# A hybrid decoder step on one core: fewer unread products, gate tiles over both PSUM pools, two output weights loaded earlier, four operand sums on another engine

## The chip, the cores and the metric

The kernel runs on one NeuronCore of a Trainium2 chip. The metric is the device time of one execution in microseconds (us). The engines are called by the names of the profile: PE (TensorE, the matrix products; PEld is its weight load), DVE (VectorE), ACT (ScalarE), POOL (GpSimd) and SP (SyncE, which here only issues transfers).

## The reference, cut to what matters

1088 tokens (1024 of a prompt and 8 sequences of 8) go through one layer, with D = 1024 and a feed-forward width of 2816:

```python
h = rmsnorm(x, pre_mix_g)
proj = h @ w_in                      # q, k, v, g of 4 retention heads; q, k, v, o of 4 mLSTM heads; 8 gate columns
ret_y = head_groupnorm(retention_chunked(q_r, k_r, v_r, S)) * silu(g_r)
ml_y = head_groupnorm(mlstm_chunked(q_m, k_m, v_m, i_pre, f_pre, C, n, m)) * sigmoid(o_m)
x = x + rmsnorm(concat(ret_y, ml_y) @ w_out, post_mix_g)
up = rmsnorm(x, pre_ffn_g) @ w_up    # then a causal convolution of width 3 over the tokens
ffn = (gelu(gate) * val) @ w_down
x = x + rmsnorm(ffn, post_ffn_g)     # the states and the last rows of `up` are outputs too
```

Everything is fp32.

## The kernel before, in words

**Tiles.** Tokens lie in the free dimension, in four blocks of 272 (`BLK`); a contraction over 1024 is eight k-tiles of 128. An fp32 product is made of three products of rounded operands: `split_to` (L141) writes the rounded part of an operand on ACT (L144) and the remainder on DVE (L146), and `dense` (L157) issues, for each k-tile, high x high, low x high and high x low (L165), 24 matmuls of 128x272 for a weight tile and a block. `load_w` (L149) brings one weight tile of 512 KB in and splits it; the high part is then named wh, the low part wl (in the output projection also woh, wol).

**The start.** `idle(n)` (L152) issues n products of a constant tile into a bank that nothing reads: 20 at the kernel's start (L239), and 3 after each of the first eight real products of the first projection (L442 passes the 3 to `dense`, which calls `idle` after each k-tile). The first projection makes two tiles of values at once. Block 0 of x becomes the operands hh (ACT, L205) and hl (DVE, L206).

**The projections** (`proj`, L431). Each of 32 weight tiles is multiplied with four blocks; each product takes a PSUM bank (by default of the pool psA, which has 2 banks; psB has 6 and serves the heads), and a callback reads the bank. For values that is a copy on ACT (L453), for q and k a rotation (`q_r`, `k_r`), for a gate tile `early_gate` (L479): DVE scales the bank into z (L484), ACT takes the sigmoid, DVE multiplies (L487). The four retention gate tiles are projected in one run (loop at L540 in `front`/`mix_head`), and among them DVE makes the mLSTM's running sums over rows of 4x1088 (`gate_rows`, L354 to L426, with scans at L383 and L394). The last four projections (L790 to L793) are those of the mLSTM gates (`late_gate`, L490, z at L497); the last one has `mix_split` (L780) as its `done`: after each block it splits the finished mixer output into the output projection's operands mh (ACT L787) and ml (DVE L788).

**The output projection** (`out_proj`, L838). All eight PSUM banks go to a new pool, psF, at L796. Eight weight tiles st_out are loaded by `load_wo` (L824), one ahead of the products and one more ahead of each; tiles 0 to 3 get buffers of their own, 4 to 7 (woh, wol) others. Each product is read on ACT (mo L847, oacc L849) and added on DVE (L851).

**The feed-forward part** is one level of Strassen's scheme: 22 tiles of gate and value, in pairs, with sums of operands. `pair_out` (L1029) makes, for each pair, the product act of gelu(gate) and value (DVE L1034), sends it to memory as bd, makes four sums of halves of it on POOL (L1042) and sends those too (L1044). `prep_a` (L1150) makes sums of the down weights wd on POOL (L1158). `halves` (L1135) splits operands for the down products: rb, read back from bd, and ra_*, from wd, on ACT (L1137) and DVE (L1138). The down products dn are L1209 to L1211.

**The order.** A scheduler orders the instructions of each engine when the kernel is built; `issue_after` only adds constraints. Each engine then runs its list strictly in order, and waits at an instruction for its inputs and its buffers.

Of the kernel before, what the change touches and what calls it, by code (L numbers as in the profile page):

```python
# [10 lines left out]
F32 = mybir.dt.float32  # L11
# [3 lines left out]
ALU = mybir.AluOpType  # L15

P = 128
D = 1024
# [74 lines left out]
def hybrid_layer_kernel(ctx: ExitStack, tc: tile.TileContext, a: dict, o: dict):  # L93
# [47 lines left out]
    def split_to(x, hi, lo, eng=nc.vector, after=None):  # L141
        act, dve = after or (None, None)
        with tc.issue_after(act.ins) if act else nullcontext():
            nc.scalar.activation(hi, x, AF.Copy)  # L144
        with tc.issue_after(dve.ins) if dve and eng is nc.vector else nullcontext():
            eng.tensor_tensor(lo, x, hi.bitcast(F32), ALU.subtract)  # L146
        return hi, lo
# [9 lines left out]
    def dense(ps, w, x, b, term=None, wait=0):  # L157

        hi, lo = w
        for k in range(KT):  # L160
            ws = slice(k * P, (k + 1) * P)
            xh, xl = (t[:, k % 4, qcols(b)] for t in x[b // 2][k // 4])
            for i, (u, v) in enumerate(((hi, xh), (lo, xh), (hi, xl))):
                if term in (None, i):
                    nc.tensor.matmul(ps, u[:, ws], v, start=k == i == 0, stop=k == KT - 1 and i == 2)  # L165
            idle(wait)
# [72 lines left out]
    idle(20)  # L239
# [191 lines left out]
    def proj(*jobs, mid=None, done=None, banks=lambda i, b: psA, terms=None):  # L431

        ws = [j[2] if len(j) > 2 else load_w(a["wi"][j[0]], f"in{j[0]}") for j in jobs]
        for b in range(4):
# [5 lines left out]
            if b == 0:  # L440
                for i, term in terms or ():
                    dense(pss[i], ws[i], h, b, term, 3 if i == term == 0 else 0)  # L442
# [64 lines left out]
    def mix_head(hd, ml):  # L507
# [15 lines left out]
        else:  # L523
# [12 lines left out]
            if hd == 0:  # L536
# [3 lines left out]
                for i in range(NH):  # L540
                    proj((12 + i, early_gate(i)))
# [238 lines left out]
    def mix_split(b):  # L780
# [3 lines left out]
        for k in range(0, KT, 2):  # L784
            hi, lo = (t[:, k % 4:k % 4 + 2, qcols(b)] for t in mx[b // 2][k // 4])
            x = yT[k // 2][:, :, o0:o0 + n]
            nc.scalar.activation(hi, x, AF.Copy)  # L787
            nc.vector.tensor_tensor(lo, x, hi.bitcast(F32), ALU.subtract)  # L788
# [4 lines left out]
    proj((31, late_gate(7)), done=mix_split)  # L793
# [18 lines left out]
    wtag = [0]  # L812
# [9 lines left out]
    wo = []  # L822

    def load_wo():  # L824

        m = len(wo)
        if m in (4, 6):
            wx.extend(slot(m + 4 + i, f"wo{'hl'[i]}{m}").rearrange("p k n -> p (k n)") for i in range(2))
        if m < 4:
            wo.append(load_w(a["wo"][m], f"out{m}", *wtile()))  # L830
        elif m < KT:
            hi, lo = (t[:, m % 2 * D:(m % 2 + 1) * D] for t in wx[-2:])
            wo.append(split_to(stage_w(a["wo"][m], f"out{m}"), hi, lo))

    wx = []
# [193 lines left out]
    def pair_out(j, ug, uv):  # L1029
# [11 lines left out]
        for o_, x, y in ((e0, e1, e0), (e1, o1, e1), (o1, o1, e0), (o0, o0, o1)):  # L1041
            nc.gpsimd.tensor_tensor(o_, x, y, ALU.subtract)  # L1042
# [343 lines left out]
```

## Time and profile before

| | |
|---|---|
| median of 3 runs (lowest to highest) | 1390.55 us (1388.64 to 1392.19) |
| the profiled execution's own time | 1391.41 us |
| its span in the profile | 1389.6 us |
| mean granted TensorE clock | 0.993 |
| PE busy | 1355.2 us (98%), 10633 products |
| DVE, ACT, POOL busy | 1006.3 us (72%), 596.1 us (43%), 445.6 us (32%) |

Busy times count what an engine executes; a wait is idle time ahead of an instruction, put down to what released it. The windows view cuts the span into stretches and gives for each the busy time of every engine and the granted clock, PEclk, as a share of 2.4 GHz: 0.50 is the lower level, 1.2 GHz, all through. Adjacent products overlap in the timeline: one takes some 0.29 us and the next begins some 0.125 us after it.

### The profile page before, as it was taken

What the parts mean: (1) busy time and instruction counts of PE and PEld (TensorE: products, weight loads), DVE (VectorE), ACT (ScalarE), POOL (GpSimd) and SP (SyncE); (2) the same over time, 40 slices, a digit from 0 to 9 for tenths busy, and PEclk for the clock granted to TensorE, in tenths of its full rate; (3) what the DMA queues carried; (4) which work ended last, traced back from release to release, by engine and by line L of the source; (5) the groups of instructions that cost most, each with busy time, mean ns of one, the idle gap of its engine ahead of it and who ended that gap; (6) DMA issues with size and microseconds to landing.
All of it is one profiled execution on the core that took longest, in us unless ns stands there. A gap on an engine that the chain in (4) does not pass through costs nothing.

```text
span 1389.6 us, 27023 instructions
## 1 busy us (share of the span) xinstructions
PE 1355.2 (98%) x10633; PEld 1329.6 (96%) x10633; DVE 1006.3 (72%) x2009; ACT 596.1 (43%) x1107; POOL 445.6 (32%) x571
## 2 busy tenths in 40 slices
PE   9999999999999999899899999999999999999995
PEld 9999999999999999899899999999999999999995
DVE  6786775476374366467989878778777787896677
ACT  7443433312222235446464434344334354553553
POOL 0444440388666000000343322221222206782000
PEclk9999999999999999999999999999999999999998
DMA  6433441376886210433224444433444458533363
GB/s 240 137 122 116 162 139 46 111 230 209 189 174 206 63 48 31 158 99 96 93 79 147 140 148 140 140 126 122 141 148 138 135 165 286 179 114 96 93 214 129
DMA packets 93167, 192.82 MB, mean 139 GB/s; under 512 B 16240, under 2 KB 41456, under 8 KB 92528
## 3 DMA queue, kind: packets, MB, share of 16 engines
q1 hardware_dynamic: 80736, 149.03, 33.1%
q0 software_dynamic: 12160, 41.95, 10.5%
q8 instruction: 84, 1.38, 0.4%
q14 instruction: 43, 0.35, 0.1%
q10 hardware_dynamic: 144, 0.11, 0.0%
HBM read 134.58 MB, written 56.47 MB: 137 GB/s over the span
## 4 chain that ended last, share of the span: by engine, by line
PE 86%; DVE 7%; ACT 3%; DMA 2%; issue 2%; SPq 0%; DVEq 0%; ACTq 0%
PE in L165 25%; PE up_S L1014 6%; PE up_S L1013 6%; PE up_S L1012 6%; PE out L165 5%; PE dn L1211 5%; PE dn L1209 5%; PE dn L1210 4%; PE up_A L1013 4%; PE up_A L1012 4%; PE up_A L1014 4%; DMA x<-in_x 1%; PE up_A L1057 1%; PE up_A L1058 1%; PE up_A L1056 1%
## 5 line engine op out<-in xcount | busy, mean ns | idle before, releaser
L165 PE MATMUL in<-hh,wh_in 128*128 128x272 f32 x1024 | 301.9, 296 | 5.2 <-DVE z L484 4.0
L165 PE MATMUL in<-hh,wl_in 128*128 128x272 f32 x1024 | 297.3, 293 | 0.0
L165 PE MATMUL in<-hl,wh_in 128*128 128x272 f32 x1024 | 296.7, 292 | 0.0
L165 PEld LDWEIGHTS in<-hh,wh_in 128*128 128x128 f32 x1024 | 193.4, 189 | 8.5 <-DVE z L484 2.7
L165 PEld LDWEIGHTS in<-hh,wl_in 128*128 128x128 f32 x1024 | 193.2, 190 | 5.4 <-issue 5.1
L165 PEld LDWEIGHTS in<-hl,wh_in 128*128 128x128 f32 x1024 | 192.8, 189 | 0.8 <-issue 0.8
L144 ACT ACTIVATE wh_up<-st_up 128x1024 fp32r<-128x1024 f32 x84 | 80.6, 959 | 170.2 <-PE up_S L1013 104.4
L1138 DVE TENSOR_TENSOR rb<-rb 128x544 fp32r<-128x544 f32 x78 | 74.7, 963 | 40.9 <-ACT rb L1137 40.4
L146 DVE TENSOR_TENSOR wl_up<-st_up,wh_up 128x1024 fp32r<-128x1024 f32 x84 | 94.7, 1127 | 9.6 <-ACT wh_up L144 9.6
L986 DVE TENSOR_TENSOR Uv<-Uv,up_S 128x272 f32<-128x272 f32 (+1 forms) x200 | 66.8, 376 | 47.3 <-PE up_S L1014 47.3
L1042 POOL TENSOR_TENSOR act<-act 128x544 f32<-128x544 f32 x44 | 70.3, 1598 | 77.4 <-DMA bd<-act 52.8
L736 POOL TENSOR_TENSOR tab<-tab 128x256 f32<-128x256 f32 x104 | 79.4, 774 | 14.3 <-DMA tab<-in_wu 9.8
L1158 POOL TENSOR_TENSOR wd<-wd 128x512 f32<-128x512 f32 x44 | 72.0, 1663 | 32.8 <-DMA wd<-in_wd 19.9
L1137 ACT ACTIVATE rb<-rb 128x544 fp32r<-128x544 f32 x78 | 50.5, 650 | 73.2 <-DMA rb<-bd 64.5
L1027 DVE SCALAR_TENSOR_TENSOR c<-Uv,vec,c 128x1024 f32<-128x1024 f32 (+1 forms) x88 | 70.2, 800 | 8.9 <-ACT c L1025 8.9
L977 POOL MEMSET Ug<- 128x2 f32 x22 | 2.2, 99 | 227.8 <-DVE yT L500 111.3
L736 POOL TENSOR_TENSOR wq<-wq 128x256 f32<-128x256 f32 x56 | 54.5, 984 | 44.7 <-DMA wq<-in_wu 42.4
L1027 DVE SCALAR_TENSOR_TENSOR c<-Ug,vec,c 128x1024 f32<-128x1024 f32 x88 | 67.5, 807 | 1.5 <-ACT c L1025 1.5
L736 POOL DMA_DIRECT2D tab<-in_wu x52 | 36.8, 713 | 79.1 <-DVE k_r L468 59.6
L1025 ACT ACTIVATE c<-Ug,vec 128x1024 f32<-128x1024 f32 (+1 forms) x44 | 34.6, 834 | 47.1 <-DVE Ug L990 44.4
L146 DVE TENSOR_TENSOR wl_in<-st_in,wh_in 128x1024 fp32r<-128x1024 f32 (+2 forms) x33 | 40.9, 1238 | 14.5 <-ACT wh_in L144 14.4
L1014 PE MATMUL up_S<-T1h,wl_up 128*128 128x272 f32 x160 | 46.6, 292 | 0.0
(547 smaller groups left out, 4678.7 us busy)
## 6 DMA issues: line engine op xcount, KB each, us to landing
rb<-bd SPq DMA_DIRECT2D x76, 272.0 KB, 2.9
st_up<-sd SPq DMA_DIRECT2D x40, 512.0 KB, 3.9
bd<-act SPq DMA_DIRECT2D x33, 544.0 KB, 4.6
st_in<-in_wi SPq DMA_DIRECT2D x31, 512.0 KB, 4.2
tab<-in_wu POOLq DMA_DIRECT2D x52, 256.0 KB, 5.2
sd<-tab POOLq DMA_DIRECT2D x26, 512.0 KB, 3.8
st_up<-in_wu SPq DMA_DIRECT2D x24, 512.0 KB, 3.6
wd<-in_wd SPq DMA_DIRECT2D x44, 256.0 KB, 4.2
```

The source lines that it names most:

```text
L144: nc.scalar.activation(hi, x, AF.Copy)
L146: eng.tensor_tensor(lo, x, hi.bitcast(F32), ALU.subtract)
L165: nc.tensor.matmul(ps, u[:, ws], v, start=k == i == 0, stop=k == KT - 1 and i == 2)
L736: last["sums"] = f(*args)
L1012: nc.tensor.matmul(ps, wh[:, c], xh[:, k, n], start=k == 0, stop=False)
L1013: nc.tensor.matmul(ps, wh[:, c], xl[:, k, n], start=False, stop=False)
L1014: nc.tensor.matmul(ps, wl[:, c], xh[:, k, n], start=False, stop=k == 3)
L1027: nc.vector.scalar_tensor_tensor(c, u(i), cw(i), c, ALU.mult, ALU.add)
L1042: nc.gpsimd.tensor_tensor(o_, x, y, ALU.subtract)
L1138: nc.vector.tensor_tensor(lo, x, hi.bitcast(F32), ALU.subtract)
L1158: nc.gpsimd.tensor_tensor(quad(p, out), quad(p, x), quad(p, y), op)
L1209: nc.tensor.matmul(t, wh[:, ms], ah, start=k == 0, stop=False)
```

## The change

Four edits:

1. 11 unread products at the start in place of 20, and 8 after the second k-tile in place of 3 after each of eight: 19 in place of 44. (The scheduler sets 16 of them ahead of the first real product and 3 behind the second.)
2. The early gate tiles take their bank from psA for blocks 0 and 2 and from psB for blocks 1 and 3.
3. Output weights 0 and 1 are loaded and split within the last gate projection, after its blocks 1 and 3. The splits of blocks 2 and 3 of the mixer output come after its last block, behind the split of weight 1. One more call of `load_wo` stands ahead of the products. Weights 4 and 5 are staged in the buffers of the up-projection's tiles in place of the weights' own staging buffers.
4. The four sums of the last pair are made on DVE in place of POOL.

```diff
@@ -141,9 +141,9 @@
     def split_to(x, hi, lo, eng=nc.vector, after=None):
         act, dve = after or (None, None)
         with tc.issue_after(act.ins) if act else nullcontext():
-            nc.scalar.activation(hi, x, AF.Copy)
+            act = nc.scalar.activation(hi, x, AF.Copy)
         with tc.issue_after(dve.ins) if dve and eng is nc.vector else nullcontext():
-            eng.tensor_tensor(lo, x, hi.bitcast(F32), ALU.subtract)
+            last["split"] = act, eng.tensor_tensor(lo, x, hi.bitcast(F32), ALU.subtract)
         return hi, lo
 
     def load_w(src, name, p=None, tag="w"):
@@ -163,7 +163,7 @@
             for i, (u, v) in enumerate(((hi, xh), (lo, xh), (hi, xl))):
                 if term in (None, i):
                     nc.tensor.matmul(ps, u[:, ws], v, start=k == i == 0, stop=k == KT - 1 and i == 2)
-            idle(wait)
+            idle(wait if k == 1 else 0)
 
     def rstd_small(out, v, w, name, shape):
 
@@ -236,7 +236,7 @@
         return tokp.tile([P, T], dt, tag="tok", name=name)[:rows, :]
 
     warm = bank(psB, P, "warm")
-    idle(20)
+    idle(11)
 
 
     h = []
@@ -439,7 +439,7 @@
                     dense(pss[-1], w, h, b)
             if b == 0:
                 for i, term in terms or ():
-                    dense(pss[i], ws[i], h, b, term, 3 if i == term == 0 else 0)
+                    dense(pss[i], ws[i], h, b, term, 8 if i == term == 0 else 0)
             if mid:
                 mid(b)
             for ps, j in zip(pss, jobs):
@@ -538,7 +538,7 @@
                 for _ in range(5):
                     next(rows)
                 for i in range(NH):
-                    proj((12 + i, early_gate(i)))
+                    proj((12 + i, early_gate(i)), banks=lambda i, b: psB if b % 2 else psA)
                     next(rows)
                     next(wsums)
                 log_exp_tables(last["sigmoid"])
@@ -777,20 +777,28 @@
 
     mx = []
 
-    def mix_split(b):
+    def mix_split(b, after=None):
         if b % 2 == 0:
             mx.append(quadrants("m", b // 2))
         o0, n = BLK[b]
         for k in range(0, KT, 2):
             hi, lo = (t[:, k % 4:k % 4 + 2, qcols(b)] for t in mx[b // 2][k // 4])
             x = yT[k // 2][:, :, o0:o0 + n]
-            nc.scalar.activation(hi, x, AF.Copy)
-            nc.vector.tensor_tensor(lo, x, hi.bitcast(F32), ALU.subtract)
+            split_to(x, hi, lo, nc.vector, after)
 
     proj((28, late_gate(4)))
     proj((29, late_gate(5)))
     proj((30, late_gate(6)))
-    proj((31, late_gate(7)), done=mix_split)
+    wo = []
+
+    def last_gate(b):
+        if b in (1, 3):
+            wo.append(load_w(a["wo"][b // 2], f"out{b // 2}"))
+            after = last["split"]
+        for i in ((0,), (1,), (), (2, 3))[b]:
+            mix_split(i, after if i > 1 else None)
+
+    proj((31, late_gate(7)), done=last_gate)
     log_exp_tables(last["sigmoid"])
     mixctx.close()
     psA = psB = pool("psF", bufs=8, space=PSUM)
@@ -809,7 +817,7 @@
     fp = pool("fp", bufs=2)
     ttile = lambda name: fp.tile([P, 3 * Q], F32, tag="t", name=name)
     utile = lambda name, i, dt=F32: fp.tile([P, UW], dt, tag="Ux"[i % 2], name=name)
-    wtag = [0]
+    wtag = [2]
 
     def wtile():
 
@@ -819,20 +827,26 @@
     mo = [[flat("mo", 2 * kh + th, k=4) for th in range(2)] for kh in range(2)]
     quarter = lambda kh, b: mo[kh][b // 2][:, :, qcols(b)]
 
-    wo = []
+    wx = []
 
     def load_wo():
 
         m = len(wo)
+        if m >= KT:
+            return
         if m in (4, 6):
             wx.extend(slot(m + 4 + i, f"wo{'hl'[i]}{m}").rearrange("p k n -> p (k n)") for i in range(2))
+        if m not in (4, 5):
+            st = stage_w(a["wo"][m], f"out{m}")
+        else:
+            st = utile(f"st_out{m}", 0)[:, :D]
+            nc.sync.dma_start(st, a["wo"][m])
         if m < 4:
-            wo.append(load_w(a["wo"][m], f"out{m}", *wtile()))
-        elif m < KT:
-            hi, lo = (t[:, m % 2 * D:(m % 2 + 1) * D] for t in wx[-2:])
-            wo.append(split_to(stage_w(a["wo"][m], f"out{m}"), hi, lo))
-
-    wx = []
+            wo.append(split_w(st, f"out{m}", *wtile()))
+        else:
+            wo.append(split_to(st, *(t[:, m % 2 * D:(m % 2 + 1) * D] for t in wx[-2:])))
+
+    load_wo()
     load_wo()
 
     def out_proj(b, steps=()):
@@ -1039,7 +1053,7 @@
         nc.sync.dma_start(out[:, HB:3 * HB], act)
         (e0, e1), (o0, o1) = [[acts_[:, i, h * HB:(h + 1) * HB] for h in range(2)] for i in range(2)]
         for o_, x, y in ((e0, e1, e0), (e1, o1, e1), (o1, o1, e0), (o0, o0, o1)):
-            nc.gpsimd.tensor_tensor(o_, x, y, ALU.subtract)
+            (nc.gpsimd if j + 1 < JT else nc.vector).tensor_tensor(o_, x, y, ALU.subtract)
         for i in range(2):
             nc.sync.dma_start(out[:, (3 + 2 * i) * HB:(5 + 2 * i) * HB], acts_[:, i, :])
```

The order moves at three places that the diff doesn't tell. Each list is one engine's, in its order; the numbers at the ends of names tell buffers apart.

On PE, the front of retention head 0 (x_r are transposes of its keys and values, s_r its scores, u_r the sums that its state S_r takes up) before, in between the gate columns of `gate_proj`, ahead of the gate tiles:

```order
L318 MATMUL gates_820<-hl_158,w_gates 128x272
L559 MATMUL x_r_1466<-cst,k_r_498 128x128
L560 MATMUL x_r_1466<-cst,v_r_263 128x128
...
L600 MATMUL s_r_1475<-q_r_497,k_r_498 128x128 x2
L559 MATMUL x_r_1480<-cst,k_r_498 128x128
L318 MATMUL gates_842<-hh_155,w_gates 128x272
L318 MATMUL gates_842<-hl_156,w_gates 128x272
```

and with the change, after the last gate tile (in_3), with the first products of head 1's q (in_0) behind it:

```order
L165 MATMUL in_3_1386<-hl_192,wh_in_1295 128x272
L559 MATMUL x_r_1441<-cst,k_r_473 128x128
L560 MATMUL x_r_1441<-cst,v_r_254 128x128
...
L600 MATMUL s_r_1450<-q_r_472,k_r_473 128x128 x2
L559 MATMUL x_r_1455<-cst,k_r_473 128x128
...
L600 MATMUL s_r_1464<-q_r_472,k_r_473 128x128 x2
L165 MATMUL in_0_1743<-hh_146,wh_in_1739 128x272
L165 MATMUL in_0_1743<-hh_146,wl_in_1740 128x272
```

The head's transposes and scores come after the gate tiles instead of before; the u_r that need them stand two blocks of head 1's q further on, ahead of the third, and the first product that reads the state (o_r) in the middle of the third.

On ACT, at the end of the last gate projection (z is its tile; L144 is with the change also the line of mh, since `mix_split` now calls `split_to`), before:

```order
L787 ACTIVATE mh_6659<-yT_814 128x2x272
L787 ACTIVATE mh_6735<-yT_813 128x2x272 x2
L144 ACTIVATE wh_out_6808<-st_out_6806 128x1024
L499 ACTIVATE z_6622<-z_6622 128x272
L101 ACT_TABLE_LOAD
L787 ACTIVATE mh_6735<-yT_814 128x2x272
L847 ACTIVATE mo_6795<-out_0_6812,vec 128x272
L787 ACTIVATE mh_6735<-yT_814 128x2x272
L849 ACTIVATE oacc_6805<-out_0_6812 128x272
L144 ACTIVATE wh_out_6841<-st_out_6839 128x1024
L144 ACTIVATE wh_out_6875<-st_out_6873 128x1024
```

and with the change:

```order
L144 ACTIVATE mh_6634<-yT_789 128x2x272
L144 ACTIVATE wh_out_6744<-st_out_6742 128x1024
L144 ACTIVATE mh_6748<-yT_786 128x2x272
...
L144 ACTIVATE mh_6750<-yT_788 128x2x272
L499 ACTIVATE z_6597<-z_6597 128x272
L101 ACT_TABLE_LOAD
L861 ACTIVATE mo_6782<-out_0_6805,vec 128x272
L861 ACTIVATE mo_6782<-out_0_6836,vec 128x272
L144 ACTIVATE mh_6750<-yT_789 128x2x272
L144 ACTIVATE wh_out_6788<-st_out_6786 128x1024
L144 ACTIVATE wh_out_6794<-st_out_6792 128x1024
L863 ACTIVATE oacc_6798<-out_0_6805 128x272
```

The split of weight 1 (wh_out) moved from behind the last projection's splits to ahead of the eight mh of blocks 2 and 3; those of weights 2 and 3 stand behind the table load, two mo and the last mh.

On DVE, the operands of the down products ahead of the product that reads the fifth rb, and the last pair's act, before:

```order
L1034 TENSOR_TENSOR act_8490<-c_8489 128x1088
L1138 TENSOR_TENSOR rb_13541<-rb_13541 128x544
L1138 TENSOR_TENSOR ra_wlo_13533<-wd_13530,ra_wlo_13533 128x512
L1138 TENSOR_TENSOR rb_13542<-rb_13542 128x544
L1138 TENSOR_TENSOR ra_whi_13534<-wd_13531,ra_whi_13534 128x512
L1138 TENSOR_TENSOR rb_13546<-rb_13546 128x544
L1138 TENSOR_TENSOR ra_dlo_13539<-wd_13528,ra_dlo_13539 128x512
L1138 TENSOR_TENSOR rb_13543<-rb_13543 128x544
```

and with the change (L1048 is the old L1034, L1152 the old L1138, L1056 the old L1042):

```order
L1048 TENSOR_TENSOR act_8465<-c_8464 128x1088
L1152 TENSOR_TENSOR rb_13516<-rb_13516 128x544
L1152 TENSOR_TENSOR ra_wlo_13508<-wd_13505,ra_wlo_13508 128x512
L1056 TENSOR_TENSOR act_8465<-act_8465 128x544
L1152 TENSOR_TENSOR rb_13517<-rb_13517 128x544
L1152 TENSOR_TENSOR ra_whi_13509<-wd_13506,ra_whi_13509 128x512
L1152 TENSOR_TENSOR rb_13521<-rb_13521 128x544
L1152 TENSOR_TENSOR ra_dlo_13514<-wd_13503,ra_dlo_13514 128x512
L1152 TENSOR_TENSOR rb_13518<-rb_13518 128x544
L1152 TENSOR_TENSOR ra_wlo_13510<-wd_13496,ra_wlo_13510 128x512
L1056 TENSOR_TENSOR act_8465<-act_8465 128x544 x2
```

Three of the four sums of act stand on DVE among these operands, two of them behind the operands that PE waits for; the fourth stands ahead, before the first row shown.

## Rows read from the trace of the kernel before

**Rows 1.** The page: busy time of PE (part 1), the chain of work that ended last by engine (part 4).
```profile
PE 1355.2 (98%) x10633; PEld 1329.6 (96%) x10633; DVE 1006.3 (72%) x2009; ACT 596.1 (43%) x1107; POOL 445.6 (32%) x571
PE 86%; DVE 7%; ACT 3%; DMA 2%; issue 2%; SPq 0%; DVEq 0%; ACTq 0%
```

**Rows 2.** Waits of PE over the whole span: the waiting tile and line, the releaser; us in total, times, the longest.
```profile
PE in L165 <- DVE z L484: 4.0, 3, 1.9
PE out L165 <- ACT woh L144: 2.3, 1, 2.3
PE out L165 <- DVE wl_out L146: 1.8, 2, 1.2
PE dn L1210 <- DVE rb L1138: 1.6, 1, 1.6
PE dn L1211 <- DVE ra_dlo L1138: 1.3, 1, 1.3
PE out L165 <- DVE z L497: 1.0, 1, 1.0
```

**Rows 3.** Windows: the stretch in us, its length, then busy time and instructions of PE, PEld, DVE, ACT, POOL, then PEclk, DMA share, GB/s.
```profile
2.00:4.00 2.00, 2.00 (x12) 2.00 (x11) 0.00 (x0) 0.68 (x2) 0.40 (x4) 1.00 0.89 258
6.00:7.00 1.00, 1.00 (x11) 1.00 (x11) 0.00 (x0) 0.35 (x1) 0.00 (x0) 1.00 1.00 388
92.00:96.00 4.00, 2.55 (x16) 2.58 (x17) 3.97 (x7) 1.46 (x4) 2.84 (x2) 0.84 0.15 36
96.00:100.00 4.00, 4.00 (x26) 4.00 (x26) 3.63 (x11) 0.00 (x0) 3.51 (x4) 0.74 0.34 123
100.00:120.00 20.00, 17.87 (x138) 17.26 (x138) 19.36 (x32) 6.20 (x10) 9.82 (x9) 1.00 0.32 108
545.00:575.00 30.00, 24.07 (x184) 23.02 (x183) 19.57 (x30) 18.95 (x33) 0.46 (x4) 1.00 0.41 137
1160.00:1165.00 5.00, 5.00 (x29) 5.00 (x29) 5.00 (x5) 1.29 (x2) 2.45 (x2) 0.69 0.79 303
```

**Rows 4.** Timeline of the start, PE and ACT: start, us, engine, line, operation, tiles and shapes, count, and in brackets the idle time before it and its releaser.
```profile
1.06 7.05 PE L155 MATMUL warm<-ones 128*128 128x128 f32 x40 [1.06 <-DVE ones L182]
8.74 1.76 ACT L205 ACTIVATE hh<-x,vec 128x272 fp32r<-128x272 f32 x4 [0.29 <-DMA x<-in_x]
13.65 0.83 PE L155 MATMUL warm<-ones 128*128 128x128 f32 x6
14.98 2.10 ACT L211 ACTIVATE sq<-x 128x1088 f32<-128x1088 f32 x2
18.27 0.38 ACT L453 ACTIVATE v_r<-in 128x272 f32<-128x272 f32 x1
19.33 0.29 PE L165 MATMUL in<-hh,wh_in 128*128 128x272 f32 x1
19.45 0.29 PE L165 MATMUL in<-hh,wl_in 128*128 128x272 f32 x1
```

**Rows 5.** Timeline of the gate stage, DVE and PE, columns as in rows 4.
```profile
91.68 1.27 DVE L372 TENSOR_TENSOR yT<-yT 4x1088 f32<-4x1088 f32 x1
93.45 0.36 PE L165 MATMUL in<-hh,wh_in 128*128 128x272 f32 x1 [1.92 <-DVE z L484]
```

**Rows 6.** Head 0's front from 66 to 90 us, by tile: line, engine, operation, count, shortest, median and longest ns, first and last start in us, shapes.
```profile
L559 PE MATMUL x_r<-cst,k_r x5: 271/273/273, 68.4 to 77.1; 128*128 128x128 f32 x4, 128*64 128x128 f32 x1
L688 PE MATMUL u_r<-vts,kz_r x8: 271/275/276, 74.2 to 84.3; 128*128 128x128 f32 x8
L701 DVE SCALAR_TENSOR_TENSOR S_r<-S_r,u_r x3: 269/270/272, 75.5 to 86.8; 128x128 f32<-128x128 f32 x3
```

**Rows 7.** Timeline of the first output products, ACT, DVE and PE, columns as in rows 4.
```profile
554.27 1.04 ACT L144 ACTIVATE wh_out<-st_out 128x1024 fp32r<-128x1024 f32 x1
560.34 1.06 ACT L144 ACTIVATE wh_out<-st_out 128x1024 fp32r<-128x1024 f32 x1 [0.58 <-DMA st_out<-in_wo]
561.43 1.22 DVE L146 TENSOR_TENSOR wl_out<-st_out,wh_out 128x1024 fp32r<-128x1024 f32 x1 [0.36 <-ACT wh_out L144]
568.50 1.06 ACT L144 ACTIVATE woh<-st_out 128x1024 fp32r<-128x1024 f32 x1 [3.39 <-DMA st_out<-in_wo]
552.65 0.36 PE L165 MATMUL out<-mh,wh_out 128*128 128x272 f32 x1 [0.96 <-DVE z L497]
570.87 0.39 PE L165 MATMUL out<-mh,wol 128*128 128x272 f32 x1 [0.87 <-DVE wol L146]
```

**Rows 8.** Timeline at the end of the last pair, DVE and POOL, columns as in rows 4.
```profile
1149.39 1.81 DVE L1138 TENSOR_TENSOR rb<-rb 128x544 fp32r<-128x544 f32 x1
1156.42 1.85 DVE L1138 TENSOR_TENSOR rb<-rb 128x544 fp32r<-128x544 f32 x1
1158.19 1.76 DVE L1138 TENSOR_TENSOR ra_dlo<-wd,ra_dlo 128x512 fp32r<-128x512 f32 x1
1163.27 0.71 DVE L1138 TENSOR_TENSOR rb<-rb 128x544 fp32r<-128x544 f32 x1
1154.19 3.49 POOL L1042 TENSOR_TENSOR act<-act 128x544 f32<-128x544 f32 x2
1157.65 3.43 POOL L1158 TENSOR_TENSOR wd<-wd 128x512 f32<-128x512 f32 x2
1161.43 1.37 POOL L1158 TENSOR_TENSOR wd<-wd 128x512 f32<-128x512 f32 x1 [0.35 <-DMA wd<-in_wd]
```

## The prediction, made before the changed kernel ran

> **What bounds the kernel now.** I read the page first: PE executes products for 1355.2 us, 98% of the span, and 86% of the chain that ended last lies on it [rows 1]. So only PE's own work, its waits and its clock count; DVE at 72% matters where PE waits for it. The list of PE's waits says where [rows 2]: 4.0 us in three waits for z, the read of an early gate tile; 2.3, 1.8 and 1.0 in the first output products, with 0.87 more for wol [rows 7]; 1.6 and 1.3 for operands of the down products behind the last pair. Last the windows, for the clock [rows 3]: where PE had run without a gap the column says 1.00; 92 to 96 us, with a wait of 1.92 us in it [rows 5], shows 0.84 and the next 4 us 0.74, and 1160 to 1165, behind the waits of 1.62 and 1.29, shows 0.69. Such a slow stretch costs: 0.16 x 4 + 0.26 x 4 = 1.7 us at the gates, 0.31 x 5 = 1.6 at the last pair. But 545 to 575 shows 1.00 although waits of 2.3 and 0.87 lie in it. A gap of some 2 us can cost 1.7 us of clock, and needn't.
>
> **Unread products.** 25 fewer. At the start PE issues 20 (40 records) from 1.06 to 8.11, then 3 (6 records, 0.83 us) behind each of eight real products, the last from 13.65 [rows 4]. Without them PE waits for operands: the last four hh of block 0 end at 8.74 + 1.76 = 10.5. Behind them 40 products at 0.125 us are left of this block's 48; before they ran from 14.3 to 19.33 [rows 4], now they end at about 10.5 + 5.1 = 15.6. That isn't the gain, because the next block needs the two psA banks, whose readers v_r stand on ACT behind the two sq (14.98 + 2.10 = 17.08) and a short wait. v_r began at 18.27 behind two hh; I put the bank free at 17.5 and the gain at 19.33 - 17.5 = **1.8**. Bounds: 0 if v_r stays where it is or transfers bind; 2.3 if the later banks come earlier too. What speaks against taking these products away: 12 records ran from 2 to 4 us and 11 from 6 to 7 us [rows 3], so PE started at half rate and got the full one only after some us of such products (the clock column reads 1.00 in both, the count is what shows it). The Trainium skill, "TensorE: Matmul & The Clock Gate", Part 1, says that TensorE starts at the lower level and that activity releases it; the counts agree, and by it the thinner start could fall back. Sixteen products before the first real one still end near 6.9. A slow stretch of 1.7 us behind them would let the block end at 17.3, still ahead of v_r, so by rule and row alike the sum is the same, until a second one comes.
>
> **Gate tiles over both pools.** Before, the tile of block b+2 of the run of gate tiles needs the bank that the z of block b frees. DVE is busy 19.36 of 20 us there [rows 3], with row operations of 1.27 us between [rows 5], so z comes late: by 1.92 at most. Now a bank is used again two tiles later, and a tile takes 24 x 0.125 = 3.0 us: a z may come 6 us later. The 4.0 us of waits go, and the 1.7 of clock behind the first. What is late next is DVE itself: it must do in 5.7 us less what it did in that time. Its share there shrinks, because head 0's front leaves this stage (the first order list of the change): three updates of S_r at 0.27 [rows 6], and the kz, pt and vx with them, all told a few us. In its new place that front stands in PE's list among blocks of head 1's q. From x_r to u_r it took 74.2 - 68.4 = 5.8 us [rows 6]; now two blocks, 6.0 us, lie between, so it just fits, with less room for the states behind; I deduct 0.5. Taken **5.2**, between 3 (DVE gives some back) and 5.7.
>
> **Output weights.** Before, the stage lost 1.8 + 2.3 + 0.87 us waiting for weights (5.0), and 1.0 for z [rows 2, 7]. The first product began at 552.65, three us each. Weight 1 was split from 554.27 [rows 7], behind the mh; now it is done before the first product ends. But the splits of weights 2 and 3 now stand on ACT behind the table load, two mo and the last mh (the second list), and the second mo needs the second product, which ends at 552.65 + 6.0 = 558.7. From there mo 0.4, mh 0.7, wh 1.06 and wl 1.22 follow: wl of weight 2 comes at about 561.9, so a **new wait of 3.2 us** takes the place of the two for wl_out. Weights 4 and 5 are issued earlier, and the waits for woh and wol at 568.5 to 571 go. The fifth product ended at 573.75 by the timeline (570.87 + 23 x 0.125); now at 561.9 + 3 x 3.0 = 570.9, gain 2.9. A gap of 3.2 us is longer than those that cost 1.6 to 1.7 of clock, so I deduct 1.7: **1.2**. Bounds: 4 (no slow stretch and the wait shorter by one) and -0.5 (wait longer by 1.7).
>
> **Last pair's sums.** Before, while POOL runs its sums (1154.19 to 1161), DVE's 128x544 operands take 1.81 us; at 1163.27, POOL idle, 0.71 [rows 8]. The two that PE waits for, rb and ra_dlo, end at 1158.27 and 1159.95 after five in a row of 1.8. Three POOL sums of 1.75 lie in that stretch. Without them POOL's remaining sums of wd fit into some 60% of it. I take three of the seven operands from 1149.39 on as short (3 x 1.1 = 3.3 us saved) and one sum of 0.7 on DVE among them (the third list: the other two stand behind): ra_dlo at 1156.4 to 1157.3, against 1158.7 when PE wants it without the first wait. Both waits go, 2.9 us, and the slow stretch behind them, 1.6; I take **4.4** of 4.5. Bounds: 2.0 (one wait stays) to 4.6. The sums that were left on POOL have no customer before the transfers of act, which come later and have some 5 us of room.
>
> **Sum.** 1.8 + 5.2 + 1.2 + 4.4 = 12.6 us, 0.9%. The profiled execution took 1391.41, so 1378.8; it stands 0.86 above the median, from which the sum gives 1377.9. I forecast **1378.5 us**. About 0.3% (4.2 us) is what a measurement of this kernel tells from no change.
>
> **Rivals.**
> *A: no clock is lost in the output stage and the start gives all.* For: 545 to 575 lost none with two waits [rows 3]. Against: a gap of 3.2 is the longest of all. 1391.4 - (2.3 + 5.7 + 4 + 4.6) = 1374.8, from the median 1373.9. Chance 0.15.
> *B: DVE and POOL stay in each other's way.* If POOL fills the stretch with its sums of wd, every operand of DVE still takes 1.8, and the sum inserted adds 1.8: ra_dlo ends at 1161.7 instead of 1159.95. The tail then loses 1.8 instead of gaining 4.4: 12.6 - 4.4 - 1.8 = 6.4, 1385.0. For: six sums of wd stand on POOL in a row. Against: POOL waited for their transfers (the one at 1161.43 did [rows 8]), so it can't fill the stretch. The Trainium skill, "Perfetto Trace Analysis", Optimizing Scalar/DVE Operations, says that GpSimd and DVE share a read port, so that moving operations between the two might not help; 0.71 against 1.81 agrees with the port, and this rival is what the rule would give. Chance 0.15.
> *C: what was gained is lost behind it,* the tail's 4.4 in the stage of wd sums that follows, or the start's 1.8 and the gates' 5.2 in head 1's q and k. 1391.4 - 8.2 to - 5.6: 1383.2 to 1385.8. Chance 0.15.
> *D, slower: the head's front in PE's list.* Head 0's x_r to its last S_r took 87.1 - 68.4 = 18.7 us [rows 6], under gate work before; now some 11 us of blocks lie among it, and 7.7 of it could stand as a wait with a slow stretch of 1.7 behind, 9.4 per head; the order of heads 1 and 2 moves too. Three heads lose 28, less 12.6: 1406. It decides from 5.6 us per head on (12.6 + 4.2 over 3). Against: between x_r and u_r the blocks cover the 5.8 us; that chain ran beside DVE at 97%. Chance 0.05.
> *E: a part doesn't do what it says,* the scheduler having put the waits elsewhere, two parts at once: within 4 us of before, 1388. Chance 0.05.
>
> **Chances.** Forecast 0.45, A 0.15, B 0.15, C 0.15, D 0.05, E 0.05. Faster by over 0.3% are the forecast, A, and nearly all of B and C: 0.86. Within 0.3% E and the rest of B and C: 0.09. Slower D: 0.05. The range takes in A (1373.9, down to 1373 for the spread of runs) and B and C with the low bounds of a term (up to 1386); D and E are left out.
>
> **What would show it.** Right: no wait for z L484 on the list of PE's waits; a new wait for wl_out of weight 2 of some 3 us near 559 less what came before, and none for woh; no wait for ra_dlo behind the last pair, its rb at 0.7 in part; 92 to 100 and 1160 to 1165 at clock 1.00; the second block of the first projection beginning near 17.5. Wrong: waits for vts, kz or S_r in PE's list behind the gates, DVE operands still at 1.8 before the down products, or a new wait in the stage behind.

## The result

The changed kernel took 1374.67 us in the median of 6 runs (1374.24 to 1376.19), the kernel before 1388.93 (1384.9 to 1392.19) beside it: ratio 0.9901, 95% interval 0.9883 to 0.9920, which is 11 to 16 us less. In later runs of the same program it was 0.9887 (0.9862 to 0.9912). The forecast was 1378.5, range 1373 to 1386, faster. One run of all those below, with edit 3 alone, took 1641.66 us at a granted clock of 0.75 and is left out of every comparison.

The profiled execution took 1375.41 us, span 1373.6, clock 0.993; that of before 1391.41 and 1389.6. Lines of the changed file stand 14 higher behind the output projection. PE's waits after the change, to be held against [rows 2] (those at the two ends of the span left out); the waiting tile and line, the releaser, us in total, times, the longest:

```profile
PE out L165 <- ACT wh_out L144: 2.6, 2, 2.1
PE ssqb_po L192 <- DVE oacc L865: 2.3, 2, 1.8
PE in L165 <- ACT v_r L453: 1.5, 2, 1.4
PE ssqb_pf L192 <- DVE xr L895: 1.1, 1, 1.1
PE out L165 <- DVE z L497: 0.6, 1, 0.6
PE dn L1225 <- DVE ra_dlo L1152: 0.2, 1, 0.2
```

The three waits for z L484 are gone, those for wl_out, woh and wol too; wh_out is new, and of the 2.9 us for rb and ra_dlo 0.2 is left. The windows, columns as in [rows 3]:

```profile
92.00:96.00 4.00, 4.00 (x34) 4.00 (x33) 3.60 (x10) 0.78 (x2) 0.67 (x1) 1.00 0.57 219
96.00:100.00 4.00, 4.00 (x34) 4.00 (x34) 3.84 (x5) 1.13 (x2) 0.74 (x2) 1.00 0.41 135
100.00:120.00 20.00, 20.00 (x162) 20.00 (x161) 18.84 (x33) 6.37 (x11) 11.55 (x11) 1.00 0.32 106
548.00:556.00 8.00, 5.42 (x27) 5.08 (x28) 6.09 (x7) 5.62 (x9) 0.19 (x2) 0.79 0.84 316
654.00:660.00 6.00, 5.45 (x29) 5.22 (x30) 4.39 (x6) 0.12 (x1) 3.03 (x1) 0.72 0.55 178
1140.00:1145.00 5.00, 4.79 (x38) 4.59 (x37) 5.00 (x7) 1.27 (x3) 1.70 (x1) 1.00 0.91 291
1350.00:1355.00 5.00, 5.00 (x29) 4.96 (x28) 3.57 (x7) 2.50 (x7) 0.00 (x0) 0.66 0.09 33
```

PE runs through 92 to 120 without a gap and at full clock. But three slow stretches stand at new places: behind the new wait (548 to 556), and at 654 and 1350, where nothing was edited. The one at 654 follows the wait for oacc of 1.8 us, which every trace has, and which is followed by a slow stretch in 4 of the 14.

Where the time went is read by setting the same product of both traces side by side (start of the product in us; the lead is before minus after):

| the same product of PE | before | after | lead | gained since the row above |
|---|---|---|---|---|
| first sum product (ssqb) of block 0 | 38.47 | 35.85 | 2.62 | 2.6 start |
| first output product | 552.65 | 541.67 | 10.98 | 8.4 gates and heads |
| last output product | 658.47 | 646.43 | 12.04 | 1.1 output weights |
| first down product | 1135.38 | 1121.78 | 13.60 | 1.6 unedited |
| 182nd down product | 1162.66 | 1144.93 | 17.73 | 4.1 last pair |
| last down product | 1375.31 | 1359.81 | 15.50 | -2.2 unedited |
| end of the span | 1389.6 | 1373.6 | 16.0 | 0.5 |

### The profile page after: what moved, and what is told of

Same layout as the page of the kernel before. It is cut to its first block, busy times and chain, and to the rows that moved or that the text cites. A ratio compares the mean times of both kernels' runs of the same rounds, so it can differ in the third digit from the quotient of the medians.

```text
span 1373.6 us, 26916 instructions
## 1 busy us (share of the span) xinstructions
PE 1348.8 (98%) x10583; PEld 1323.9 (96%) x10583; DVE 1009.7 (74%) x2013; ACT 596.3 (43%) x1107; POOL 440.8 (32%) x567
## 4 chain that ended last, share of the span: by engine, by line
PE 90%; DVE 4%; ACT 3%; DMA 1%; issue 1%; SPq 0%; DVEq 0%; ACTq 0%
PE in L165 27%; PE up_S L1028 6%; PE out L165 6%; PE up_S L1027 6%; PE up_S L1026 6%; PE dn L1223 5%; PE dn L1225 5%; PE dn L1224 4%; PE up_A L1027 4%; PE up_A L1026 4%; PE up_A L1028 4%; ACT hh L205 1%; PE up_A L1071 1%; PE up_A L1072 1%; PE up_A L1070 1%
## 5 line engine op out<-in xcount | busy, mean ns | idle before, releaser
L144 ACT ACTIVATE wh_up<-st_up 128x1024 fp32r<-128x1024 f32 x84 | 80.6, 960 | 160.6 <-PE up_S L1027 98.3
L1152 DVE TENSOR_TENSOR rb<-rb 128x544 fp32r<-128x544 f32 x78 | 74.3, 957 | 34.2 <-ACT rb L1151 33.7
L736 POOL TENSOR_TENSOR tab<-tab 128x256 f32<-128x256 f32 x104 | 84.1, 819 | 9.3 <-DMA tab<-in_wu 4.7
L1056 POOL TENSOR_TENSOR act<-act 128x544 f32<-128x544 f32 x40 | 63.1, 1577 | 61.0 <-DMA bd<-act 33.1
L736 POOL TENSOR_TENSOR wq<-wq 128x256 f32<-128x256 f32 x56 | 50.3, 908 | 48.3 <-DMA wq<-in_wu 46.1
```

What stands on the lines that cost most here:

```text
L144: act = nc.scalar.activation(hi, x, AF.Copy)
L736: last["sums"] = f(*args)
```

## The experiments

Each was run in five rounds beside the kernel before; ratios are to that kernel, and 0.001 is 1.4 us.

### Each edit alone, on the kernel before

Edit 1 alone:

```diff
-    idle(20)
+    idle(11)
-            idle(wait)
+            idle(wait if k == 1 else 0)
-                    dense(pss[i], ws[i], h, b, term, 3 if i == term == 0 else 0)
+                    dense(pss[i], ws[i], h, b, term, 8 if i == term == 0 else 0)
```

> The kernel before with edit 1 alone (19 unread products in place of 44). Theory S (the four edits act each at its place and their gains add): the first q product starts some 2.9 us earlier, as it does with all four edits, and the whole is 2 to 4 us faster than before. Rival G (DVE limits the gate stage, so an earlier start is given back there): the start is 2.9 us earlier but the waits for z grow, and the whole is within 1 us of before.

Ratio 0.9990 (0.9975 to 1.0005): no change that is clear. The start led by 2.5 us. Of that, 1.7 were left at the first output product and -1.7 at the last one. Two waits were longer than before, the one for z and the one for weights:

```profile
PE in L165 <- DVE z L484: 5.1, 4, 2.2
PE out L165 <- ACT woh L144: 3.1, 1, 3.1
```

Against 4.0 and 2.3 [rows 2] that is 1.9 us. The weight behind woh was issued 1.7 us earlier than before, but took 8.2 us to land instead of 7.4, and so landed 0.9 earlier (567.56 against 568.47). The rest went to a slow stretch at 568 to 575 (clock 0.58), where before had none. The time is what G forecast. That the start made the wait for z grow is not shown: with edit 4 alone, whose start is that of before, z L484 has 5.0 us in 4 waits as well.

Edit 2 alone:

```diff
-                    proj((12 + i, early_gate(i)))
+                    proj((12 + i, early_gate(i)), banks=lambda i, b: psB if b % 2 else psA)
```

> The kernel before with edit 2 alone (early gate tiles over both pools). Theory S: no wait for z L484 (before: 4.0 us in 3), no slow stretch at 92 to 100; the stage ends 6 to 7 us earlier and the whole is 6 to 8 us faster than before. Rival D (head 0's front then waits in PE's list): new waits for kz, vts or S_r of some us, whole 0 to 3 us faster.

Ratio 0.9939 (0.9924 to 0.9955), 8.5 us. No wait for z, none for kz, vts or S_r, clock 1.00 from 84 to 130; from 300 us on to the output products it leads by 7 to 8.5. S holds, D does not. Head 0's front moves behind the gate tiles with this edit alone (its first x_r at 122.27, before at 68.41). It also gave back 2.4 at 560 to 567 to a slow stretch (clock 0.58) and gained 3.4 behind the last pair, where one of the two waits was missing (ra_dlo 1.2 alone) and the slow stretch too, with no edit there.

Edit 3 alone (the hunks of `split_to`, `mix_split`, `last_gate`, `load_wo` and `wtag`):

```diff
-    proj((31, late_gate(7)), done=mix_split)
+    proj((31, late_gate(7)), done=last_gate)
...
-    wtag = [0]
+    wtag = [2]
```

> The kernel before with edit 3 alone (two output weights loaded in the last gate projection). Theory S: the first output products end 1 us earlier net: a wait of 2 to 3 us for wh_out of weight 2 in place of 5.9 us in five waits, with or without a slow stretch of 1.6; whole 1 to 3 us faster. Rival W (the new wait eats the gain): whole within 1 us of before.

Ratio 0.9969 (0.9957 to 0.9982), 4.3 us; more than S. In the profile the output products themselves gained 0.2 net, since a slow stretch at 558 to 566 took 2.4 (the lead is 1.5 us at the first of them and 1.7 at the last). But here too the last pair's waits shrank to 0.4 us with its sums on POOL, and the lead grew by 4.0 there, with no edit; so this profile doesn't show where the 4.3 us of the runs come from.

Edit 4 alone:

```diff
-            nc.gpsimd.tensor_tensor(o_, x, y, ALU.subtract)
+            (nc.gpsimd if j + 1 < JT else nc.vector).tensor_tensor(o_, x, y, ALU.subtract)
```

> The kernel before with edit 4 alone (the last pair's four sums on DVE). Theory S: no waits for rb L1138 and ra_dlo L1138 behind the last pair (2.9 us before), clock 1.00 there; whole 3.5 to 4.5 us faster. Rival B (DVE and POOL stay in each other's way): the operands of DVE still take 1.8 us and the waits stay; whole within 1 us of before or up to 2 slower.

Ratio 0.9980 (0.9968 to 0.9991), 2.8 us. No wait for rb or ra_dlo; the lead grows from 1.45 at the first down product to 5.99 at the 181st, 4.5 as S said. The runs gave less; a likely reason is that the wait is not in every run of before, since it isn't in every run with the sums on POOL, as the next pair shows.

### The last pair: what the four sums cost where

Edit 4 undone in the changed kernel:

```diff
-            (nc.gpsimd if j + 1 < JT else nc.vector).tensor_tensor(o_, x, y, ALU.subtract)
+            nc.gpsimd.tensor_tensor(o_, x, y, ALU.subtract)
```

> The changed kernel with edit 4 undone (the last pair's four sums on POOL again). Theory S (the tail's gain of 4.1 us is edit 4's): waits for rb L1152 and ra_dlo L1152 of 2 to 3 us behind the last pair come back with a slow stretch of 1.6; 3 to 4.5 us slower than the changed kernel, ratio to before about 0.993. Rival P (those waits hang on when the wd transfers land, and vanish with the earlier edits, as with edits 2 and 3 alone, which left 1.2 and 0.4): waits of at most 1.2 us, 0 to 2 us slower than the changed kernel, ratio 0.990 to 0.9915.

Ratio 0.9917 (0.9897 to 0.9937), median 1378.09, runs from 1374.87 to 1382.89. The profiled execution was the fastest of these (1374.87) and shows no such wait at all; the slowest is 8 us above it, where the changed kernel's 6 runs lie within 2. So P holds for that execution, S for the mean: the wait comes and goes from run to run. In this trace the same sums on POOL were held up by transfers, and DVE's operands beside the gaps were short:

```profile
1140.56 1.65 POOL L1172 TENSOR_TENSOR wd<-wd 128x512 f32<-128x512 f32 x1 [0.69 <-DMA wd<-in_wd]
1143.24 3.16 POOL L1056 TENSOR_TENSOR act<-act 128x544 f32<-128x544 f32 x2 [1.04 <-DMA bd<-act]
1140.37 0.68 DVE L1152 TENSOR_TENSOR ra_whi<-wd,ra_whi 128x512 fp32r<-128x512 f32 x1
1142.70 0.68 DVE L1152 TENSOR_TENSOR ra_dlo<-wd,ra_dlo 128x512 fp32r<-128x512 f32 x1
```

In the trace of before POOL had no such gap from 1148.60 to 1161.1, and all eight operands that DVE began in that time took 1.8 us ([rows 8] has three of them).

Then the changed kernel with as many sums on POOL that nobody reads, at the old place:

```diff
+        if j + 1 == JT:
+            for i in range(4):
+                c = cs_[:, i % 2, :]
+                nc.gpsimd.tensor_tensor(c[:, :HB], c[:, :HB], c[:, HB:2 * HB], ALU.subtract)
```

> The changed kernel, in which POOL also makes four sums of 128x544 at the place where it made the last pair's, in and out of a buffer that nobody reads any more. Theory C (the operands on DVE are late because POOL's sums hold them up): rb and ra_* take 1.8 us again beside these sums, waits of 1 to 3 us come back ahead of the down products, up to a slow stretch more; 1 to 4 us slower than the changed kernel. Rival O (only what POOL's results were late for counted, that is the transfers of act): no waits, time of the changed kernel within 0.7 us.

Median 1379.49, six runs in two groups: 1373.19, 1373.68, 1376.62 and 1382.35, 1382.88, 1383.29. The profiled one is of the upper group (1383.29); PE's waits there:

```profile
PE dn L1228 <- DVE rb L1156: 5.0, 1, 5.0
PE dn L1229 <- DVE ra_dlo L1156: 1.1, 1, 1.1
```

That is twice what C allowed, and a slow stretch stands there too (1146 to 1156 at 0.50); DVE has its own four sums here besides.

DVE's operands in that execution (its own sums of act left out), and what POOL ran beside them (start, us, engine, line, operation):

```profile
1138.84 0.71 DVE L1156 TENSOR_TENSOR rb<-rb 128x544 fp32r<-128x544 f32 x1
1139.48 1.85 DVE L1156 TENSOR_TENSOR ra_wlo<-wd,ra_wlo 128x512 fp32r<-128x512 f32 x1
1143.06 1.78 DVE L1156 TENSOR_TENSOR rb<-rb 128x544 fp32r<-128x544 f32 x1
1144.77 1.81 DVE L1156 TENSOR_TENSOR ra_whi<-wd,ra_whi 128x512 fp32r<-128x512 f32 x1
1146.51 1.85 DVE L1156 TENSOR_TENSOR rb<-rb 128x544 fp32r<-128x544 f32 x1
1148.28 1.75 DVE L1156 TENSOR_TENSOR ra_dlo<-wd,ra_dlo 128x512 fp32r<-128x512 f32 x1
1139.06 3.49 POOL L1060 TENSOR_TENSOR c<-c 128x544 f32<-128x544 f32 x2 [1.29 <-DVE act L1048]
...
1144.23 3.54 POOL L1060 TENSOR_TENSOR c<-c 128x544 f32<-128x544 f32 x2
```

and the same operands in the changed kernel:

```profile
1139.60 0.68 DVE L1152 TENSOR_TENSOR ra_wlo<-wd,ra_wlo 128x512 fp32r<-128x512 f32 x1
1140.21 0.71 DVE L1056 TENSOR_TENSOR act<-act 128x544 f32<-128x544 f32 x1
1140.84 0.71 DVE L1152 TENSOR_TENSOR rb<-rb 128x544 fp32r<-128x544 f32 x1
1141.48 0.68 DVE L1152 TENSOR_TENSOR ra_whi<-wd,ra_whi 128x512 fp32r<-128x512 f32 x1
1142.08 0.71 DVE L1152 TENSOR_TENSOR rb<-rb 128x544 fp32r<-128x544 f32 x1
1142.71 0.68 DVE L1152 TENSOR_TENSOR ra_dlo<-wd,ra_dlo 128x512 fp32r<-128x512 f32 x1
1137.47 1.63 POOL L1172 TENSOR_TENSOR wd<-wd 128x512 f32<-128x512 f32 x1 [0.67 <-DMA wd<-in_wd]
1142.84 1.70 POOL L1172 TENSOR_TENSOR wd<-wd 128x512 f32<-128x512 f32 x1 [3.74 <-DMA wd<-in_wd]
```

With POOL busy every operand but one takes 1.8 us; with POOL idle from 1139.1 to 1142.8, waiting for a transfer, 0.7. Nobody reads the sums that were put back, so it is their running that delays DVE, in this execution: C, not O. The lower group has the times of the changed kernel; it was not profiled. What sets the group was not separated; the landing of the transfers, for which POOL waits between its sums in the trace of edit 4 undone, is the likely cause and was only argued.

### The gates: banks, or the work that moved

In the changed kernel head 0's front stands behind the gate tiles, so DVE has less to do there. To tell that from the banks, the change was kept but for the banks, and the front held at its new place (`last["gate"]` is the last product of the gate tiles; the lines that set it are left out here):

```diff
-                    proj((12 + i, early_gate(i)), banks=lambda i, b: psB if b % 2 else psA)
+                    proj((12 + i, early_gate(i)))
...
-                nc.tensor.transpose(px[:n, 0, i, :], k[:, csl(c)], ident)
-                nc.tensor.transpose(px[:n, 1, i, :], v[:, csl(c)], ident)
+                with tc.issue_after(last["gate"].ins) if hid == 0 else nullcontext():
+                    nc.tensor.transpose(px[:n, 0, i, :], k[:, csl(c)], ident)
+                    nc.tensor.transpose(px[:n, 1, i, :], v[:, csl(c)], ident)
```

> The changed kernel with edit 2 undone (early gate tiles from psA alone), but with the transposes of head 0 held behind the last gate tile, where the changed kernel has them. Theory K (the banks remove the waits for z): waits for z L484 of 2 us or more stay and cost, with a slow stretch, 3 to 6 us against the changed kernel; ratio to before 0.993 to 0.995. Rival F (it was head 0's front, moved off DVE's busiest stage, that removed them): no or under 1 us of waits for z, the time of the changed kernel within 1 us.

Ratio 0.9954 (0.9936 to 0.9972), some 8 us above the changed kernel.

```profile
PE in L165 <- DVE z L484: 5.1, 2, 3.5
```

K holds: with the front out of the way but two banks, PE waits 5.1 us for z, loses 3.4 to the clock (0.57 over 86 to 94), and its first output product comes 8.3 us later than the changed kernel's (549.93 against 541.67). That is more than K's 3 to 6. Moving the front gained nothing; the banks are what the gain needs. Whether they would do it with the front at its old place was not run.

This trace has one thing more: with the four sums on DVE it still shows 0.8 and 1.3 us of waits for rb and ra_dlo behind the last pair. Among the eight traces with edit 4 that add no sums on POOL it is the only one with more than 0.2, so the edit makes that wait rare and not impossible.

### The start and the weights, undone

The changed kernel with 44 unread products again:

```diff
-    idle(11)
+    idle(20)
-            idle(wait if k == 1 else 0)
+            idle(wait)
-                    dense(pss[i], ws[i], h, b, term, 8 if i == term == 0 else 0)
+                    dense(pss[i], ws[i], h, b, term, 3 if i == term == 0 else 0)
```

> The changed kernel with edit 1 undone (44 unread products again). Theory K (the 2.9 us that the start gains are kept, once the waits for z and for weights, which gave them back in the kernel with edit 1 alone, are gone): 2 to 4 us slower than the changed kernel, ratio to before 0.992 to 0.993. Rival G (the start's gain is given back behind it in this kernel too): within 1 us of the changed kernel, ratio 0.990.

Ratio 0.9896 (0.9875 to 0.9918), 1375.62, not told apart from the changed kernel. Its first output product comes at 544.08, 2.4 us behind the changed kernel's and 1.4 behind that of its second profiled execution (542.66, below), so most of the start's gain is kept up to there, as K said. In this trace 1.6 of it comes back at once, because the profiled execution has no slow stretch behind the same wait of 2.6 us.

With none:

```diff
-    idle(11)
+    idle(0)
-                    dense(pss[i], ws[i], h, b, term, 8 if i == term == 0 else 0)
+                    dense(pss[i], ws[i], h, b, term, 0)
```

> The changed kernel with no unread products at all. Theory V (the second block waits for v_r on ACT at 17.15 us; a slower start is hidden by the 1.4 us of that wait, and beyond it costs): the first block runs at half rate in part, the q projection starts 0 to 3 us later, 0 to 3 us slower than the changed kernel. Rival Z (the start is bound by the operands alone): the same time as the changed kernel within 0.5 us, the second block at 17.2.

Ratio 0.9885 (0.9863 to 0.9907), 1374.09, again the changed kernel's time. PE begins at 4.73 and waits 7.0 us for hh in two waits instead of running unread products. From 8 to 16 us it starts 39 products, 46 with the change: without unread ones its products stand 0.23 us apart from 10.5 to 13.6, instead of 0.125. But the second block begins at 17.06, where it began at 17.15 behind a wait of 1.4 for v_r, and the first sum product at 36.06 (35.85): the slower start is hidden by that wait but for 0.2 us, V's way, and the time is Z's.

The same shows with 19 unread products. In the trace of edit 4 undone, whose start is that of the changed kernel, the clock fell at the start (columns as in [rows 3]):

```profile
10.00:12.00 2.00, 1.96 (x10) 1.73 (x10) 1.51 (x4) 1.90 (x4) 0.00 (x0) 0.69 1.03 402
12.00:14.00 2.00, 2.00 (x10) 2.00 (x10) 2.00 (x5) 2.00 (x6) 0.00 (x0) 0.50 1.04 416
```

The second block began at 17.22 even so, and the first sum product came at 36.29, 0.4 later than in the changed kernel.

With edit 3 undone:

```diff
-    proj((31, late_gate(7)), done=last_gate)
+    proj((31, late_gate(7)), done=mix_split)
...
-    wtag = [2]
+    wtag = [0]
```

> The changed kernel with edit 3 undone (output weights 0 and 1 loaded as before). Theory S (edit 3's gain is the waits for weights alone): waits of 4 to 6.5 us for wl_out, woh and wol in place of 2.6 for wh_out, 1 to 3 us slower than the changed kernel, ratio to before 0.991 to 0.992. Rival M (more rests on it, since the landing of the weights bounds the stage and an earlier start is given back there): 3.5 to 6 us slower, ratio 0.9925 to 0.9945.

Ratio 0.9934 (0.9911 to 0.9958), 0.0040 above the mean of the changed kernel's two, 5.6 us. The waits are those of before (1.2, 0.63, 2.3, 0.87), and a slow stretch stands behind them (558 to 567 at 0.62). M by its size, but not for M's reason: the lead that this kernel loses in the output products is 3.8 us, 2.4 of it waits (5.0 against 2.6) and the rest clock. The transfers moved with the stage: the first woh is split 15.8 us behind the first output product, as before.

### The new wait

```diff
-        for i in ((0,), (1,), (), (2, 3))[b]:
-            mix_split(i, after if i > 1 else None)
+        for i in ((0,), (1,), (2,), (3,))[b]:
+            mix_split(i, after if i > 2 else None)
```

> The changed kernel with the mixer's block 2 split after its own block again (only block 3 behind the split of weight 1). Theory A (the new wait of 2.6 us at the first output products is ACT's queue: eight mh, z, table load, mo, then the split of weight 2): ACT has four mh less there, weight 2 is split 1 to 2.5 us earlier, the wait falls to 0 to 1.5 us; 1 to 3 us faster than the changed kernel. Rival L (weight 1 is then split later, behind block 2's splits, and the wait moves to the second product or to z): within 1 us of the changed kernel.

Ratio 0.9887 (0.9869 to 0.9906), median 1373.69. Waits of the output products:

```profile
PE out L165 <- ACT wh_out L144: 1.4, 2, 0.8
PE out L165 <- DVE z L497: 1.0, 1, 1.0
```

The wait fell by 1.2 us and that for z rose by 0.4, so A holds in the profile, with a little of L; the runs don't resolve 1 us. In the changed kernel ACT is busy without a gap from 541.09 to 550.9:

```profile
541.09 1.06 ACT L144 ACTIVATE wh_out<-st_out 128x1024 fp32r<-128x1024 f32 x1 [0.70 <-PE in L165]
542.05 3.93 ACT L144 ACTIVATE mh<-yT 128x544 fp32r<-128x544 f32 x7
545.88 0.42 ACT L499 ACTIVATE z<-z 128x272 f32<-128x272 f32 x1
546.31 1.28 ACT L101 ACT_TABLE_LOAD   x1
547.61 0.88 ACT L861 ACTIVATE mo<-out,vec 128x272 f32<-128x272 f32 x2
548.39 0.65 ACT L144 ACTIVATE mh<-yT 128x544 fp32r<-128x544 f32 x1
548.93 1.99 ACT L144 ACTIVATE wh_out<-st_out 128x1024 fp32r<-128x1024 f32 x2
```

### The same program twice

> The changed kernel once more, unaltered. Theory L (waits are the same in each execution of a program, but whether a slow stretch of PE's clock follows a wait is not): the same waits within 0.3 us in the profile, v_r 1.4, wh_out 2.6, ssqb 5 to 6 in all, but at least one slow stretch gone, added or elsewhere, and with it up to 1.6 us between the two profiled executions. Rival N (the slow stretches belong to the program): slow stretches at the first output products, behind 655 and at 1352 again, and the two profiled executions within 0.5 us.

Its profiled execution took 1372.35 us, 3.1 less than the first; waits 2.6 for wh_out, 1.8 for v_r, 0.6 for z, 2.3 for oacc, as before within 0.3, though xr had 2.2 instead of 1.1. The 3.1 is also more than L's 1.6, as all three slow stretches are gone. Its windows at the places of the first one's slow stretches:

```profile
548.00:556.00 8.00, 5.36 (x39) 4.81 (x38) 6.52 (x9) 7.12 (x12) 0.09 (x1) 1.00 0.71 267
654.00:660.00 6.00, 6.00 (x46) 5.92 (x47) 4.33 (x5) 1.64 (x4) 3.53 (x2) 1.00 0.60 178
1350.00:1355.00 5.00, 5.00 (x42) 5.00 (x41) 4.47 (x7) 1.04 (x3) 0.00 (x0) 1.00 0.00 0
```

All at 1.00: the same wait of 2.6 us cost a slow stretch in one execution and none in the other. L holds in kind. Of all seven traces with this wait of 2.6 us, five have a slow stretch behind it.

The wait for xr tells what such a stretch is worth. PE reaches it 21 us behind the wait for oacc. In the four traces with a slow stretch between the two it is 1.1 us, in the other ten 2.2 to 2.3: of the 1.7 us that the clock takes there, PE would have waited 1.2 for DVE anyway.

## Why the prediction was right, point by point

**As a whole** it was right: faster, in the range. It was 4 us too high, and the result lies at rival A's time (1373.9), partly for A's reasons: the start gave more than its bound, and the output stage lost clock in the first profiled execution, as forecast, and none in the second. The term that was mis-sized is that of the gates, 5.2 for 8.4 measured, beyond its bound of 5.7.

**Unread products, 1.8:** the second block began at 17.15 behind v_r, as worked out (17.5), and the place gained 2.2 there and 2.6 by the first sum product, beyond the bound of 2.3, because the wait for the next v_r shrank too. What it is worth in the whole is less: nothing clear alone, and at most some 2 us in the changed kernel, which the runs don't tell from none. The two profiled executions without a slow stretch among their products (44 products and the changed kernel again) stand 2.1 us apart, 1374.45 against 1372.35; the medians 1 to 2. That a slow stretch at the thinner start would cost next to nothing held in the trace that had one (0.4 us), and even with no unread product at all.

**Gates, 5.2:** right in mechanism, too small. Measured in the trace: 8.4 to the first output product, 6.9 of it assigned: z L484 4.0, q_r, k_r and the mLSTM's yt_m 0.9, z L497 0.3, clock 1.7. The step that failed is the deduction of 0.5 for head 0's front, which waited for nothing, and the waits for q_r and k_r behind it, which went too and were in no term. Most of the other 1.5 us goes with the waits: the product that waited 0.48 us for q_r at 140.78 began 0.77 behind the one before it, and the next 0.23 behind it, where 0.125 is usual, so each wait that went was worth some 0.25 us more than it is listed with. In the second execution the place had 7.4 (542.66), since two waits for yt_m, 0.5 us, came back there. Edit 2 alone gave 8.5 us, and without it 0.0060 is lost, 8.3.

**Output weights, 1.2:** the place gave 1.1 with the new wait (2.6 forecast as 3.2, for wh instead of wl; the four durations that the forecast adds, 0.4, 0.7, 1.06 and 1.22, make 3.4) and a slow stretch. In the second execution, with the same wait and no slow stretch, the products took 1.6 us less (103.2 against 104.8). Alone and undone the edit is worth more, 4.3 and 5.6. Behind these waits a long slow stretch stands in three of the five profiles with the old weights (568 to 575, 560 to 567, 558 to 567), but not in before's, from which the term was taken; with the new weights none is as long but in edit 3 alone (558 to 566). So the term was sized on an execution that had been spared, which fits the larger gain in the runs; the sizes over the runs were not taken apart further.

**Last pair, 4.4:** 4.1 in the trace. ra_dlo ended at 1143.4, which is 1157.0 on the times of before and within the 1156.4 to 1157.3 worked out. Over the runs the edit gave 3 us, for the wait comes and goes with the sums on POOL: the trace with edit 4 undone gained 4.6 at this place without it. B's way, that DVE stays slow beside POOL, didn't happen, since POOL stood idle for a transfer from 1139.1 to 1142.8; when POOL was kept busy there, it did, and the upper group of runs took 8 to 9 us more. The sentence of the Trainium skill, "Perfetto Trace Analysis", Optimizing Scalar/DVE Operations, agrees on the port (0.7 against 1.8) and not on the outcome here: moving the sums helped, as it takes POOL off while DVE is behind.

**Rivals:** C came about for edit 1 alone, in part. D did not: no wait for kz, vts or S_r.

**Clock:** the first two profiled executions compared happen to have three slow stretches each among their products, so the 16 us are not luck of the clock; but most of the 1.6 us forward (1.2 by the shorter wait for xr) and of the 2.2 us back (1.7 by the stretch at 1350) in the unedited stages is.

## What to carry to other kernels

An edit that removes a wait is worth what the next wait behind it does not take back: run each edit alone and also undone from the whole, since the start's 2.6 us were nothing clear alone and at most some 2 in company. A profile is one execution: before sizing a gain on a wait in it, see whether other runs have that wait. More buffers between an engine and a reader that lags by bursts gained 8 us where moving work off the reader gained none. Where VectorE is on the path, count what GpSimd runs beside it, not only what it produces.

## What the runs showed of the hardware

- A slow stretch of PE's clock is not the program's: behind the same wait of 2.6 us in the output products it stood in one profiled execution of the changed kernel and not in the other, and all three of the first were missing in the second: 1375.41 against 1372.35 us. It followed in five of the seven traces that have this wait. Behind the four waits of the old weights it lasted longer where it came (560 to 567 us at 0.58, in three of five traces).
- A slow stretch ahead of a wait for a slower engine costs less than its 1.7 us: behind the one at 654 the wait for xr was 1.1 us, and 2.2 to 2.3 in all ten traces without one there.
- The changed kernel's runs lie 2 and 4 us apart (6 runs each), those of before 7 (6 runs) to 10 (11 runs). That it is the fewer waits is not shown: `split2_in_place`, with less waiting still, spread over 5.
- A DVE operation of 128x512 or 128x544 with two inputs takes 0.7 us, or mostly 1.8 when one of POOL's sums of that size runs beside it.
